# x loaded transposed, and the root and the shift of the first norm put on after the q, k and v products

## The chip, the cores and the metric

The kernel runs on one core of one Trainium2 chip. A core has five engines with a queue each: TensorE (PE, matrix products, with its weight loads counted apart as PEld), VectorE (DVE), ScalarE (ACT), GpSimd (POOL) and SyncE (SP), which here only issues DMA transfers. Data lie in SBUF (128 partitions); products land in the eight banks of PSUM. The metric is device microseconds of one execution. The kernel before takes 1100.62 us, the median of three runs between 1099.32 and 1101.92.

## The reference, cut to what matters

One decoder layer on a sequence of 1024 rows of width 1024, float32 throughout. The change concerns the start of its first half:

```python
mod = c_act @ w_ada[l] + b_ada[l]                    # c_act = silu(c), one vector
sh1, sc1, g1, sh2, sc2, g2 = split(mod, 6)
h = rmsnorm(x, pre_w_mix[l]) * (1.0 + sc1) + sh1     # rmsnorm: x * rsqrt(mean(x*x) + EPS) * w
proj = h @ w_in[l]
aq, ak, av, hq, hf, hi, hg = split(proj)             # 512, 128, 128, then 4 x 512 columns
...                                                  # rotary, windowed attention on aq, ak, av
...                                                  # gated recurrence on hq, hf, hi, hg
x = x + g1 * rmsnorm(concat([attn, rec]) @ w_out[l], post_w_mix[l])
h = rmsnorm(x, pre_w_mlp[l]) * (1.0 + sc2) + sh2
x = x + g2 * rmsnorm(square(relu(h @ w_up[l])) @ w_down[l], post_w_mlp[l])
```

For one row t of h this is h[t, :] = root[t] * (x[t, :] * a) + sh1, where root is a number for each row and a = pre_w_mix * (1 + sc1) and sh1 are vectors along the width. So h @ W = root[t] * ((x * a) @ W) + sh1 @ W.

## The kernel before, in words

**Tiles.** Rows come in eight tiles `tb` of 128, and two halves `th` of four tiles. The width comes in eight blocks `kb` of 128. PE contracts over partitions, so h is needed with the width on partitions: tiles `hh[kb][th]` of 128 x 512. Each float32 operand of a large product is split in a high part (`hi`, written by ACT rounded to fp32r) and a low part (`lo`, the rest, by DVE), and a product is three: hi*hi, hi*lo, lo*hi. One row tile of q takes 24 products 512 wide, one of k and v together 24 products 256 wide.

**Before the first product** (lines 103 to 220, 337 to 374): SP loads x row by row, ACT squares and sums it, POOL takes the power -1/2 (`norm_rstd`), DVE or ACT scales the rows (`norm_scale`), PE transposes 128 x 128 pieces into PSUM (`first_T`), and `split_evac` writes the high part scaled by a and shifted by sh1 on ACT, subtracts the shift again on POOL, and writes the low part from PSUM on DVE. The scale and shift vectors come from `wada1` in pieces (`mod_mm`, `mod_fold`), for the block or two blocks that are due next. PE fills waiting time at the start with products that nobody reads (`idle`, tile `spare`).

**The first half** (lines 406 to 455): for each block, the four row tiles of half 0 get part 0 (hi*hi and hi*lo of q and kv), then part 1 (lo*hi), in six PSUM banks. **The second half** (lines 620 to 639): half 1 is transposed and split, q of tile 4 is accumulated meanwhile, and the results of tiles 0 to 3 are read out (`qproj`, `kvproj`) and rotated (`rope`).

**Attention and values** (lines 642 to 679): a loop of 16 fillers, which are q and k of tiles 4 to 7 and then `values(0..7)`, the third of the other projections, on h; between them the steps of `attention(tb)` are issued, tile 0 from filler 4 on. After it the recurrence heads, the output projection and the channel mixing follow; they take some 900 us and are not touched.

**What sets the order.** Up to line 640 `pin(True, ...)` makes every engine issue in the order of the program text. From line 640 on a planner orders each engine's queue by the order of the text among what it holds ready, but nothing goes ahead of the last pinned instruction of its engine. SP is planned throughout. Pools with a fixed number of buffers (`H` 32 tiles, `W` 6, `T2` 5, PSUM `pmm` 2, `pb` 5, `pa` 1) make a new tile wait for the release of an old one.

Line numbers in the profile are mostly 39, the helper that issues every operation, so rows are read by tile names: `x`, `xT`, `pm` (modulation), `pq` and `pk` (q and k, v products), `pv` (values), `hhi` and `hlo`, `comb` (attention scores).

Of the kernel before, what the change touches and what calls it, by code (L numbers as in the profile page):

```python
# [9 lines left out]
F32 = mybir.dt.float32  # L10
# [6 lines left out]
P = 128  # L17
# [30 lines left out]
def hybrid_layer(ctx: ExitStack, tc: tile.TileContext, I, out, dbg=None):  # L48
# [54 lines left out]
    xh = [[None, None] for _ in range(TB)]  # L103

    def load_x(tb, hfs=(0, 1)):
        for hf in hfs:
            xh[tb][hf] = (m_ if tb < 4 else hT_)(f"x{tb}_{hf}")
            SP.dma_start(xh[tb][hf], I["x"][tb * P:(tb + 1) * P, hf * 512:(hf + 1) * 512])

    load_x(0)  # L110
# [3 lines left out]
    tab = cload("tab", [P, 200], pool=tiny0, eng=POOL)  # L114
# [15 lines left out]
    prew1s = small.tile([P, KB], F32, tag="prew1s", bufs=1, name="prew1s")  # L130
# [55 lines left out]
    ssx = [small.tile([P, 4, 2], F32, tag="ssx", name=f"ssx{th}") for th in range(2)]  # L186

    def norm_sq(tb, hfs=(0, 1), eng=None):
        for hf in hfs:
            junk = t_(f"jx{tb}_{hf}")  # L190
            if eng is DVE:
                DVE.tensor_tensor(junk, xh[tb][hf], xh[tb][hf], ALU.mult)
                DVE.tensor_reduce(ssx[tb // 4][:, tb % 4, hf:hf + 1], junk, AX.X, ALU.add)
                continue
            ACT.activation(junk, xh[tb][hf], AF.Square, accum_out=ssx[tb // 4][:, tb % 4, hf:hf + 1])

    rx = {}

    def norm_rstd(th, a, b):

        if not a:
            rx[th] = small.tile([P, 4], F32, tag="rr4", name=f"r_x{th}")
        t = small.tile([P, 4], F32, tag="rs4", name=f"t_x{th}{a}")
        for i in range(a, b):
            DVE.tensor_scalar(t[:, i:i + 1], ssx[th][:, i, 0:1], ssx[th][:, i, 1:2], D * EPS, ALU.add, ALU.add)
        POOL.tensor_tensor(rx[th][:, a:b], t[:, a:b], mhalf[:, a:b], ALU.pow)

    def norm_scale(th, hf, eng, tbs=range(4)):
        for tb in tbs:
            xt = xh[4 * th + tb][hf]  # L210
            if eng is ACT:
                ACT.activation(xt, xt, AF.Copy, scale=rx[th][:, tb:tb + 1])
            else:
                DVE.tensor_scalar(xt, xt, rx[th][:, tb:tb + 1], None, ALU.mult)

    def first_T(th, kb, mk=tp_ps):
        pst = mk(f"xT{th}_{kb}")
        hf, col = kb // 4, (kb % 4) * P
# [13 lines left out]
    hh = [[None, None] for _ in range(KB)]  # L232

    def first_evac(th, kb, pst, then=None):
        hh[kb][th] = (hT_(f"hhi{kb}_{th}", F32R), hT_(f"hlo{kb}_{th}", F32R))
        c = slice(kb, kb + 1)
        split_evac(pst, a1[:, c], sh1[:, c], ns1[:, c], *hh[kb][th], f"f{th}_{kb}", then)
# [27 lines left out]
    nc.vector.memset(sel, 0.0)  # L265
    for gate in range(2):
        gs = slice(64 * gate, 64 * gate + 64)
        nc.vector.memset(sel[gs, gs], 1.0 / 32)
# [12 lines left out]
    def mod_mm(q, kps=range(4)):  # L281

        n = 256 if q[0] else P
        if kps[0] == 0:
            pm[q] = a_ps(f"pm{q[0]}_{q[1]}")
        for kp in kps:
            for i in range(4):
                w2 = wa1[q, kp, i // 2][:, i % 2 * 256:][:, :256] if q[0] else wa1[q, kp, 0][:, P * i:P * i + P]
                PE.matmul(pm[q][32 * i:32 * i + 32, :n], lhsT=csr[:, 2 * kp + i % 2, :], rhs=w2,
                          start=(kp == 0), stop=(kp == 3), tile_position=(0, 32 * i))  # L290

    def mod_copy(q):
        n = 256 if q[0] else P
        pm[q, 0] = t_(f"ms{q[0]}_{q[1]}", (P, n))
        DVE.tensor_copy(pm[q, 0], pm[q][:, :n])

    def mod_fold(q):
        n = 2 if q[0] else 1
        pst, ms = pm[q], pm[q, 0]
        for j in range(n):  # L300
            PE.matmul(pst[:, 256 + P * j:256 + P * j + P], lhsT=ms[:, P * j:P * j + P], rhs=sel, start=True, stop=True)
        s2 = small.tile([P, 2], F32, tag="m1s", name=f"m1s{q[0]}_{q[1]}")
        cols = pst[:, 256:256 + n * P].rearrange("p (n g j) -> p g n j", g=2, j=64)[:, :, :, 0]
        c = slice(2 * q[0] + q[1], 2 * q[0] + q[1] + n)
        DVE.tensor_tensor(s2[:, :n], cols[:, 1], bT[:, 8 + c.start:8 + c.stop], ALU.add)
        DVE.tensor_tensor(sh1[:, c], cols[:, 0], bT[:, c], ALU.add)
        DVE.scalar_tensor_tensor(a1[:, c], s2[:, :n], 1.0, prew1s[:, c], ALU.add, ALU.mult)
        DVE.tensor_scalar(ns1[:, c], sh1[:, c], -1.0, None, ALU.mult)

    wa1, wqr, wkvr = {}, [], []  # L310

    def load_wa(q, kp, gate=0):
        src = I["wada1"][gate, q[0], kp] if q[0] else I["wada1"][kp % 2, 0, 2 * q[1] + kp // 2]
        wa1[q, kp, gate] = load_raw(hT_, f"wa{gate}_{q[0]}{q[1]}_{kp}", src)
# [1429 lines left out]
```

## Time and profile before

| | |
|---|---|
| median of three runs | 1100.62 us (1099.32 to 1101.92) |
| profiled execution, first to last instruction | 1097.6 us; no device time of its own is listed, the median is 3.0 us more than this span |
| PE busy | 1076.2 us, 98% |
| DVE, ACT, POOL busy | 795.1, 584.6, 373.2 us |
| first product of q | 15.91 us |
| first half of the projections ends | 63.5 us |
| tiles 4 and 5 done, first attention transpose | 84.5 us |
| first values product | 112.7 us |
| first product of the recurrence heads | 197.9 us |

The page gives busy time of each engine over the span. The timeline lists merged runs of equal instructions: start, length, engine, source line, operation, output and inputs, shape, count, and in brackets the idle time before them with what ended it. The rows that the prediction reads are shown there.

### The profile page before, as it was taken

Reading aid. Unit: us, or ns where it says so; the run is one execution under the profiler, and the core shown is the slowest. Engines: PE = TensorE matmul, PEld = TensorE weight load, DVE = VectorE, ACT = ScalarE, POOL = GpSimd, SP = SyncE. Lnnn points to the kernel's source line nnn. Section 1 sums busy time; section 2 is a strip of 40 time slices with the busy share of each in tenths; the row PEclk is TensorE's granted clock in tenths of the full one; section 3 lists DMA queues with packets and bytes.
Section 4 is the critical chain, followed back from the end, with each engine's and each line's share of the span. In section 5 each row is a group of like instructions: output and inputs, shape, how many; then the busy total and the mean of one; then the engine's idle time right before and its main releaser. Section 6 shows DMA issues by size and latency. Waiting matters only on the chain.

```text
span 1097.6 us, 16208 instructions
## 1 busy us (share of the span) xinstructions
PE 1076.2 (98%) x5547; PEld 878.2 (80%) x5547; DVE 795.1 (72%) x1323; ACT 584.6 (53%) x1206; POOL 373.2 (34%) x499
## 2 busy tenths in 40 slices
PE   8999999999999999999999999999999999999995
PEld 6788776778888888888888888888888888888884
DVE  4365777878865574559776767876767787899876
ACT  3445544364565764566655555556664543555434
POOL 1153211033324663432543444533333333310014
PEclk9999999999999999999999999999999999999998
DMA  9701301534310352324577676767998888998537
GB/s 347 265 7 57 117 1 43 181 101 140 125 56 11 108 182 96 125 79 144 194 246 249 233 259 227 257 216 244 320 364 289 275 299 259 337 308 272 169 76 131
DMA packets 101587, 203.37 MB, mean 185 GB/s; under 512 B 13025, under 2 KB 13681, under 8 KB 101505
## 3 DMA queue, kind: packets, MB, share of 16 engines
q1 hardware_dynamic: 85968, 154.52, 41.4%
q0 software_dynamic: 15392, 47.57, 14.3%
q8 instruction: 43, 0.70, 0.3%
q14 instruction: 40, 0.32, 0.1%
q10 hardware_dynamic: 144, 0.26, 0.1%
HBM read 147.25 MB, written 55.05 MB: 184 GB/s over the span
## 4 chain that ended last, share of the span: by engine, by line
PE 92%; DVE 3%; ACT 1%; DMA 1%; POOL 1%; issue 1%; SPq 0%; DVEq 0%; POOLq 0%; ACTq 0%
PE pda L39 16%; PE pua L39 14%; PE pdc L39 8%; PE po L39 8%; PE puc L39 7%; PE pu L39 4%; PE pdb L39 4%; PE pq L39 4%; PE phg L39 4%; PE phq L39 3%; PE pub L39 3%; PE phf L39 3%; PE pv L39 3%; PE pk L39 2%; PE o L39 1%; PE sc L39 1%
## 5 line engine op out<-in xcount | busy, mean ns | idle before, releaser
L39 POOL TENSOR_TENSOR b<-b,b 128x512 f32<-128x512 f32 x64 | 89.6, 1400 | 222.8 <-DMA b<-w_dn 222.4
L39 ACT ACTIVATE dw<-dwr 128x512 fp32r<-128x512 f32 x72 | 45.4, 630 | 46.5 <-DMA dwr<-td 32.4
L39 ACT ACTIVATE s<-s 128x512 f32<-128x512 f32 x84 | 53.0, 631 | 31.8 <-DVE s L39 30.5
L39 DVE TENSOR_TENSOR dw<-dwr,dw 128x512 fp32r<-128x512 f32 x72 | 53.6, 744 | 9.0 <-ACT dw L39 8.9
L39 DVE TENSOR_TENSOR acc<-pda,acc 128x512 f32<-128x512 f32 x68 | 46.5, 684 | 13.7 <-PE pda L39 13.3
L39 POOL DMA_DIRECT2D td<-b x64 | 36.3, 567 | 21.6 <-POOL b L39 18.7
L39 POOL TENSOR_TENSOR rrf<-ssf,mhalf 128x1 f32<-128x1 f32 x7 | 7.9, 1253 | 95.3 <-DVE ssf L39 95.3
L39 DVE TENSOR_TENSOR wt<-s,wt 128x512 fp32r<-128x512 f32 x42 | 37.2, 886 | 2.6 <-ACT wt L39 2.5
L39 ACT ACTIVATE s<-pua 128x512 f32<-128x512 f32 x28 | 16.7, 598 | 39.4 <-PE pua L39 33.9
L39 ACT ACT_TABLE_LOAD x28 | 35.9, 1283 | 1.2 <-PEq L1737 0.7
L39 DVE SCALAR_TENSOR_TENSOR macc<-wada,cs,macc 128x512 f32<-128x512 f32 x42 | 33.7, 803 | 3.4 <-DMA wada<-wada 2.9
L39 POOL DMA_DIRECT2D b<-w_dn x64 | 34.4, 540 | 0.0
L39 POOL TENSOR_TENSOR comb<-comb,rd 128x512 f32<-128x512 f32 x8 | 11.7, 1458 | 63.3 <-DVE rd L39 44.2
L39 PE MATMUL pua<-bt_0h,wt 128*128 128x512 f32 x84 | 32.7, 389 | 0.0
L39 PE MATMUL pua<-bt_1h,wt 128*128 128x512 f32 x84 | 32.7, 389 | 0.0
L39 PE MATMUL pua<-bt_3h,wt 128*128 128x512 f32 x84 | 32.7, 389 | 0.0
L39 PE MATMUL pua<-bt_2h,wt 128*128 128x512 f32 x84 | 32.7, 389 | 0.0
L39 DVE TENSOR_TENSOR wt<-a,wt 128x512 fp32r<-128x512 f32 x42 | 31.0, 738 | 0.9 <-ACT wt L39 0.9
L39 DVE TENSOR_TENSOR acc<-pdc,acc 128x512 f32<-128x512 f32 x36 | 24.6, 684 | 8.5 <-PE pdc L39 8.4
L39 ACT ACTIVATE wt<-s 128x512 fp32r<-128x512 f32 x42 | 26.3, 626 | 8.2 <-DVE s L39 8.0
L39 PE MATMUL pda<-dw,du_6h 128*128 128x512 f32 x96 | 29.6, 389 | 0.0
L39 PE MATMUL pda<-dw,du_7h 128*128 128x512 f32 x96 | 29.5, 389 | 0.0
(757 smaller groups left out, 3746.1 us busy)
## 6 DMA issues: line engine op xcount, KB each, us to landing
dur<-ud SPq DMA_DIRECT2D x112, 256.0 KB, 4.5
wada<-wada SPq DMA_DIRECT2D x64, 256.0 KB, 3.5
b<-w_dn POOLq DMA_DIRECT2D x64, 256.0 KB, 5.2
td<-b POOLq DMA_DIRECT2D x64, 256.0 KB, 3.3
dwr<-td SPq DMA_DIRECT2D x64, 256.0 KB, 4.3
a<-w_u SPq DMA_DIRECT2D x56, 256.0 KB, 4.4
dwr<-w_dn SPq DMA_DIRECT2D x48, 256.0 KB, 4.5
ud<-s SPq DMA_DIRECT2D x42, 256.0 KB, 3.6
```

The source lines that it names most:

```text
L39: ins = op(*args, **kw)
```

## The change

x comes from the host transposed as well (`xT`, blocks of 128 x 512), so it isn't transposed on PE. q, k and v are multiplied from x times a alone. The root of each row is put on when the products are read out of PSUM, and sh1 @ W is added as one row, the same for all tiles. Sums of squares run over partitions now, so ACT squares, POOL adds eight blocks and PE sums over partitions. The other projections (values and heads) still use h: half 0 is multiplied in place by rows of roots on POOL (`h_rows`) and split (`h_split`) late, half 1 is loaded once more for it. The scale vector is computed from `wsc`, half as many tiles, and the shift vector by DVE from `wada`. Tiles 4 and 5 are done together in the second half, so the loop of fillers has 12 instead of 16, with attention from filler 1 on.

The diff, cut to its core (a line of "..." where lines are left out):

```diff
-    load_x(0)
+    BLK = {0: 1, 1: 1, 2: 2, 4: 2, 6: 2}
+    scw = {b: [] for b in BLK}
+    xw = [w_(f"xT0_{i}") for i in range(4)]
+    xT = [[xw[kb // 2][:, kb % 2 * 512:kb % 2 * 512 + 512] for kb in range(KB)], [None] * KB]
...
+    load_sc(0)
+    load_x0(0)
...
-    tab = cload("tab", [P, 200], pool=tiny0, eng=POOL)
+    tab = cload("tab", [P, 200], pool=tiny0, eng=ACT)
...
+    def square_x(th, kb):
+        if kb == 0:
+            ssq[th] = m_(f"ssq{th}")
+            ACT.activation(ssq[th], xT[th][kb], AF.Square)
+        else:
+            sq = t_(f"sqx{th}_{kb}")
+            ACT.activation(sq, xT[th][kb], AF.Square)
+            POOL.tensor_tensor(ssq[th], ssq[th], sq, ALU.add)
+
+    def x_root(th):
+        pst = tp_ps(f"ssx{th}")
         for j in range(4):
-            PE.transpose(pst[:, j * P:(j + 1) * P], xh[th * 4 + j][hf][:, col:col + P], ident)
-        return pst
+            PE.matmul(pst[:, j * P:(j + 1) * P], lhsT=ssq[th][:, j * P:(j + 1) * P], rhs=ones, start=True, stop=True)
+        t = small.tile([P, 4], F32, tag="rs4", name=f"t_x{th}")
+        DVE.tensor_scalar(t, pst.rearrange("p (j c) -> p j c", c=P)[:, :, 0], D * EPS, None, ALU.add)
+        rx[th] = small.tile([P, 4], F32, tag="rx", name=f"r_x{th}")
+        POOL.tensor_tensor(rx[th], t, mhalf[:, 0:4], ALU.pow)
+        rx8[th] = small.tile([P, 4], F32, tag="rx8", name=f"r_x8{th}")
+        DVE.tensor_scalar(rx8[th], rx[th], 0.125, None, ALU.mult)
+
+    def x_rows(th):
...
+        DVE.tensor_tensor(d3, ident.unsqueeze(1).broadcast_to([P, 4, P]), rx[th].unsqueeze(2).broadcast_to([P, 4, P]),
+                          ALU.mult)
+        pst = tp_ps(f"rbx{th}")
+        for j in range(4):
+            PE.matmul(pst[:, j * P:(j + 1) * P], lhsT=ones, rhs=dg[:, j * P:(j + 1) * P], start=True, stop=True)
+        rxb[th] = raw_(f"rxb{th}")
+        ACT.activation(rxb[th], pst, AF.Copy)
...
+    def x_split(th, kb, then=None):
...
+        ACT.activation(hi, xT[th][kb], AF.Copy, scale=a)
+        if then:
+            then()
+        DVE.scalar_tensor_tensor(lo, xT[th][kb], a, hi.bitcast(F32), ALU.mult, ALU.subtract)
+
+    def h_rows(th, kb, eng=POOL):
+        eng.tensor_tensor(xT[th][kb], xT[th][kb], rxb[th], ALU.mult)
+
+    def h_split(th, kb):
...
+        split_evac(xT[th][kb], a1[:, c], sh1[:, c], ns1[:, c], hi, lo, f"f{th}_{kb}")
...
+    def add_sh(half, ks):
+        for k in ks:
...
+                DVE.scalar_tensor_tensor(sacc[half], wt, c, sacc[half], ALU.mult, ALU.add)
+
+    def fold_sh(half):
...
+            PE.transpose(pst[:, j * P:(j + 1) * P], sacc[half][:, j * P:(j + 1) * P], ident)
...
+    def shift_mm(kind):
+        if kind == "q":
+            DVE.tensor_copy(csr, sh1.unsqueeze(2).broadcast_to([P, KB, 32]))
+        n = 512 if kind == "q" else 256
...
+                PE.matmul(pst[32 * i:32 * i + 32, :n], lhsT=csr[:, k, :], rhs=w, start=(r == 0), stop=(r == 1),
+                          tile_position=(0, 32 * i))
+        shp[kind] = t_(f"shp{kind}", (P, n))
+        ACT.activation(shp[kind], pst[:, :n], AF.Copy)
+
+    def shift_fold(kind):
...
+            PE.matmul(pst[:, j:j + P], lhsT=sel, rhs=shp[kind][:, j:j + P], start=True, stop=True)
+        shb[kind] = hv_(f"shb{kind}")[:, :n]
+        ACT.activation(shb[kind], pst[:, :n], AF.Copy, scale=0.125 if kind == "q" else 1.0)
...
-    idle(15)
...
+    idle(6)
+    mod_mm(0)
+    mod_copy(0)
     idle(2)
...
+    mod_fold(0)
     idle(4)
...
     for kb in range(KB):
...
+        square_x(0, kb)
+        if kb and b:
+            mod_mm(b)
...
-        if kb + 1 < KB:
-            xT0.append(first_T(0, kb + 1))
...
+        if kb in (2, 3, 4, 5):
+            add_sh(0, range(2 * kb - 4, 2 * kb - 2))
         if kb == 6:
...
+            fold_sh(0)
+            load_sh(1, range(4))
+            for k in range(4, KB):
+                load_x1(k)
+            load_sh(1, range(4, KB))
+        if kb >= 5:
+            for k in ((0,), (1, 2), (3,))[kb - 5]:
+                square_x(1, k)
         if kb == 7:
...
+            x_root(0)
+            add_sh(1, range(4))
         for tb in range(4):
             first_mm(kb, tb, 1)
...
+        ACT.activation(q, pq, AF.Copy, scale=rx8[tb // 4][:, tb % 4:tb % 4 + 1])
...
+            DVE.tensor_scalar(kv, pk, r, None, ALU.mult)
...
+            DVE.scalar_tensor_tensor(kv, pk, r, shb["k"], ALU.mult, ALU.add)
...
+    def shift_q(tb):
+        POOL.tensor_tensor(qn[tb], qn[tb], shb["q"], ALU.add)
+
+    def shift_kv(tb):
+        POOL.tensor_tensor(kvn[tb], kvn[tb], shb["k"], ALU.add)
...
+    for kb in range(KB):
+        x_split(1, kb)
+        if kb == 0:
+            qproj(0)
+            qproj(1)
+            pq0 += [mm_ps("pq4"), mm_ps("pq5")]
+            pk45 = tp_ps("pk45")
+            pk0 += [pk45[:, 0:256], pk45[:, 256:512]]
+        if kb in (1, 2):
+            for tb in (2 * kb - 2, 2 * kb - 1):
+                kvproj(tb)
+        if kb == 1:
+            qproj(2)
+            qproj(3)
+        if kb < 4:
+            square_x(1, kb + 4)
+        if kb == 1:
+            x_rows(0)
+        if kb < 4:
+            add_sh(1, (kb + 4,))
+        if kb == 4:
+            fold_sh(1)
+        if kb == 5:
+            x_root(1)
+            shift_mm("q")
+            shift_mm("k")
+        if kb == 6:
+            shift_fold("q")
+            shift_fold("k")
+            x_rows(1)
+        if kb >= 3:
+            h_rows(0, kb - 3)
+        for part in range(2):
+            for tb in (4, 5):
+                first_mm(kb, tb, part)
+    for tb in range(4, 6):
+        qproj(tb)
+        kvproj(tb)
     for tb in range(4):
         eng = DVE if tb < 2 else POOL
+        shift_kv(tb)
+        rope(tb, 2, eng)
+        shift_q(tb)
         rope(tb, 8, eng)
-        rope(tb, 2, eng)
     pin(False, ACT, DVE, POOL, PE)

     def filler(i):
-        if i < 8:
-            (kvproj if i % 2 else qproj)(4 + i // 2)
-            rope(4 + i // 2, 2 if i % 2 else 8)
+        if i < 4:
+            (kvproj if i % 2 else qproj)(6 + i // 2)
+            if i == 0:
+                for kb in range(5, KB):
+                    h_rows(0, kb)
+            for kb in (2 * i, 2 * i + 1):
+                h_split(0, kb)
+            shift_q(4 + i)
+            rope(4 + i, 8)
+            rope(4 + i, 2)
+            if i == 3:
+                for k in range(KB):
+                    load_x1(k, hv_)
         else:
-            values(i - 8)
+            values(i - 4)
+            if i < 8:
+                for kb in (2 * i - 8, 2 * i - 7):
+                    h_rows(1, kb)
+                    h_split(1, kb)
...
-    att_a = (4, 5, 6, 7, 8, 9, 10, 11)
-    mod_a = (12, 13, 15)
-    for i in range(16):
+    att_a = (1, 2, 3, 4, 5, 6, 7, 8)
+    mod_a = (8, 9, 11)
+    for i in range(12):
```

More of the change, by code (lines that the diff above doesn't have):

```diff
@@ L183, in modrow @@
         POOL.tensor_tensor(t[:, hs], t[:, hs], wt, ALU.mult)
[L186 to L214, printed above, removed]
@@ L264, in hybrid_layer @@
     sel = XA.tile([P, P], F32, tag="sel", name="sel")
[L265 to L268, printed above, removed]
+    nc.vector.memset(sel, 1.0 / 32)
     def hv_(name):
```

258 lines of the change are left out of this document (119 added, 139 removed).

## The prediction

> **What bounds the kernel now.** I read the page first, then busy time by stage, then the merged timeline and the chain of waits of the first 85 us.
>
> ```profile
> span 1097.6 us, 16208 instructions
> PE 1076.2 (98%) x5547; PEld 878.2 (80%) x5547; DVE 795.1 (72%) x1323; ACT 584.6 (53%) x1206; POOL 373.2 (34%) x499
> 0.00:15.90 15.90, 12.54 (x71) 8.82 (x71) 6.47 (x26) 7.81 (x20) 2.76 (x8) 1.00 0.89 306
> 15.90:63.50 47.60, 47.59 (x370) 38.31 (x371) 20.77 (x52) 20.27 (x40) 7.53 (x10) 1.00 0.68 254
> 63.50:84.50 21.00, 20.39 (x124) 17.18 (x123) 12.82 (x37) 8.38 (x13) 15.25 (x39) 1.00 0.05 14
> 84.50:112.70 28.20, 27.86 (x216) 23.10 (x215) 18.86 (x43) 16.29 (x56) 9.23 (x21) 1.00 0.21 65
> ```
>
> The last four rows are stages (width; busy PE, weight load, DVE, ACT, POOL; granted clock; DMA). PE is the bound: from 15.9 us on it hardly pauses, so a change pays in two ways only: PE work that goes, and PE waits that come or go. POOL and DVE have room in the second row, and POOL is 15.25 of 21.0 in the third.
>
> **The start.** Timeline rows of PE, ACT and POOL, and the table of DMA issues:
>
> ```profile
> 1.65 5.99 PE L39 MATMUL spare<-spare,ones_r 128*128 128x512 f32 x15 [1.65 <-DVE spare L121]
> 9.08 2.31 PE L39 MATMUL spare<-spare,ones_r 128*128 128x512 f32 x9
> 13.06 0.64 PE L39 MATMUL pm<-wa,csr 128*32 128x128 f32 x16
> 15.91 0.50 PE L39 MATMUL pq<-wq0h,hhi 128*128 128x512 f32 x1 [0.38 <-ACT hhi L39]
> 3.40 0.63 ACT L39 ACTIVATE jx<-x 128x512 f32<-128x512 f32 x1 [1.16 <-DMA x<-x]
> 13.48 0.63 ACT L39 ACTIVATE wq0h<-wqr 128x512 fp32r<-128x512 f32 x1 [2.48 <-DMA wqr<-w_q]
> 1.31 0.73 POOL L39 DMA_DIRECT2D c_tab<-tab  x1 [0.86 <-POOLq L1737]
> c_tab<-tab POOLq DMA_DIRECT2D x1, 100.0 KB, 5.0
> ```
>
> The first tile is there at 3.40, wq0, the thirteenth on SP's queue, at 13.48: 0.84 a tile. After the change two scale tiles, one of x and wq0 lead, so wq0 is there at 3.40 + 3 x 0.84 = 5.9. `c_tab`, there at 1.31 + 5.0 = 6.3 now, moves to ACT's queue: between 3.4 (like the first tile) and 6.3; I take 4.0, since it shares the engines with two tiles. I allow 0.8 for the three small steps of silu: the first scale products start at 4.8, take one 0.64 row, and from the end of `pm` to the first `pq` it was 15.91 - 13.70 = 2.2. First product 7.6 instead of 15.9: **-8.3**, with 7.0 to 9.9 as its ends. Square sums, root and scaling of x leave this path; the squares move behind the products.
>
> Fifteen spare products took 0.40 each, nine later ones 0.26, at a granted clock of 1.00 in the rows: PE's first microseconds run slower. Twelve spare products and a gap replace 31. If that rate lasted as long after the new first product, the loss is at most 15 x 0.40 - 15 x 0.23 = 2.6; at least 0. I take **+0.6**, as most of the slow time is still spent on spares. [...]
>
> **The first half, 15.9 to 63.5.** Prices, from the chain of waits and the timeline:
>
> ```profile
> 18.03 1.01 PE pm L39 x32
> 22.25 1.00 PE pm L39 x16
> 27.44 0.45 PE pm L39 x4
> 27.89 0.44 PE xT L39 x4
> 73.31 2.88 PE pk L39 x24
> 76.19 5.47 PE pq L39 x24
> ```
>
> PE loses nine sets of transposes, 9 x 0.44 = 4.0; half of the modulation products, 0.5 in the second part (1.01) and 1.0 in each of three quarters (two rows like 22.25 become one), 3.5. It gains `fold_sh`, four transposes 0.44, and `x_root`, four full products at 0.45 / 2 = 0.22, 0.9. **-6.2**; the half ends at 7.6 + 0.6 + 41.4 = 49.6, not 63.5. DMA keeps ahead: 60 tiles were loaded here, 60 are now (16 scale, 16 shift, 16 x, 12 weights), and a block needs half the modulation tiles. DVE gets eight additions of the shift and POOL seven to ten of the squares: hidden, since a low part is due only 2.8 (eight `pq` at 5.47 / 24 = 0.23, eight `pk` at 0.12) after its block starts; uncovered, each is one of the rows below.
>
> **The second half, tiles 4 and 5, 63.5 to 84.5.** More prices:
>
> ```profile
> 34.20 2.56 ACT L39 ACTIVATE x<-x,r_x 128x512 f32<-128x512 f32 x4
> 211.31 3.11 DVE L39 SCALAR_TENSOR_TENSOR macc<-wada,cs,macc 128x512 f32<-128x512 f32 x4
> 8.82 0.69 DVE L39 TENSOR_TENSOR jx<-x 128x512 f32<-128x512 f32 x1
> 72.65 1.40 DVE L39 COPY kv<-pk 128x256 f32<-128x256 f32 x4
> 8.57 0.31 DVE L39 COPY csr<-cs 128x256 f32<-128x256 f32 x1
> 73.35 0.60 ACT L39 ACTIVATE q<-pq 128x512 f32<-128x512 f32 x1 [2.18 <-PE pq L39]
> 56.71 1.02 POOL L39 TENSOR_TENSOR r_x<-t_x,mhalf 128x4 f32<-128x4 f32 x1 [2.46 <-DVE t_x L39]
> L39 POOL TENSOR_TENSOR b<-b,b x64: 1282/1302/1965, 565.1 to 963.4; 128x512 f32<-128x512 f32 x64
> ```
>
> PE work: q and k of two tiles 2 x (5.47 + 2.88) = 16.7; two `x_rows` and `x_root` 2.7; `fold_sh` 0.4; `shift_mm` q at twice the 1.00 row, 2.0, and k 1.0; `shift_fold` six products, 1.35. 24.2. Then waits, all from orders pinned in the code:
> - `x_root(0)` stands before the last low-part products (1.4), and its read, power (1.02) and 1/8 take about 1.4. Only then does ACT read q0 (0.60) and free the bank of pq4: 0.6.
> - DVE has four shift additions (2.8) and the first low part (0.78) queued behind that root; PE gets to it after 0.6 + 1.4: 1.6.
> - `x_rows(0)` is ahead of block 1 on PE. Its diagonal stands on DVE behind one more addition, a low part and two kv reads: 0.78 + 0.78 + 0.70 + 0.69 - 0.70 of PE work = 2.2.
> - in block 5 `shift_mm` waits for root, 1/8 and `csr`: 0.2 + 1.02 + 0.2 + 0.31 = 1.7.
>
> That is 6.1. A sharing comes on top; POOL and DVE, timeline:
>
> ```profile
> 564.83 0.68 DVE L39 TENSOR_TENSOR wt<-s,wt 128x512 fp32r<-128x512 f32 x1
> 565.09 1.58 POOL L39 TENSOR_TENSOR b<-b,b 128x512 f32<-128x512 f32 x1 [3.96 <-DMA b<-w_dn]
> 565.55 1.67 DVE L39 TENSOR_TENSOR s<-a,s 128x512 f32<-128x512 f32 x1
> ```
>
> POOL's addition, 1.30 by the median, took 1.58 while a DVE instruction with two SBUF operands ran, and the next DVE one took 1.67 instead of 0.68, ending 0.55 after POOL. They exclude each other; DVE lost 1.0, POOL 0.28. Low parts read PSUM and SBUF before; now `x_split` reads x and the high part, both SBUF, as the shift additions do, while POOL adds squares and multiplies rows. Queue against queue: POOL's additions for blocks 4 and 5 fall into the second and third wait (+1.2 each), the next two and the first rows delay the low part of block 3 and the last shift addition (+0.5, +1.35). Waits 10.4, end at 49.6 + 24.2 + 10.4 = 84.2, against 80.0 without it. I take 84.2: the rows show it. So **+13.6** on the stage's 21.0. [...]
>
> **The attention stage, from 84.5.** Its PE work stays (28.2 to the first `pv`), but two banks now come free at once: **+0.6** for one ACT read. POOL is what runs late:
>
> ```profile
> 15.96 0.70 POOL L39 TENSOR_SCALAR f<-hhi,ns 128x512 f32<-128x512 f32 x1 [3.62 <-ACT hhi L39]
> 76.22 0.57 POOL L39 TENSOR_TENSOR rt<-q,c_cosT 128x128 f32<-128x128 f32 x1
> 78.57 0.25 POOL L39 TENSOR_TENSOR kv<-rt 128x32 f32<-128x32 f32 x1
> 80.31 0.95 POOL L39 MEMSET comb<- 128x1024 f32 x1
> 93.59 1.48 POOL L39 TENSOR_TENSOR comb<-comb,rd 128x512 f32<-128x512 f32 x1 [7.62 <-ACT q L39]
> 183.27 1.06 PE L39 MATMUL pT<-c_tab,comb 128*128 128x128 f32 x8 [0.42 <-DVE comb L39]
> 201.59 0.49 PE L39 MATMUL rb<-dg,ones 128*128 128x128 f32 x2 [0.45 <-DVE dg L39]
> 73.97 0.55 DVE L39 TENSOR_TENSOR rt<-q,c_cosT 128x128 f32<-128x128 f32 x1
> 77.23 0.20 DVE L39 TENSOR_TENSOR kv<-rt 128x32 f32<-128x32 f32 x1
> ```
>
> One tile's ropes take POOL 76.22 to 78.82, 2.6 (eight instructions). From the shift rows (4.5 before the second half ends, 79.7) it has four shifts of q and k (1.30, and half of it for the 256 columns of k: 4 x 1.95) and two ropes, 13.0; then three row products 3.9, eight `h_split` steps 5.6, three q shifts 3.9, three ropes 7.8, the memset 0.95 and two `comb` 3.0: 38.2, to 117.9, and 0.75 for the last low part, 118.6. The first values tile wants that one after 21 of its 24 products (4.8), at 84.2 + 0.6 + 28.2 + 4.8 = 117.8: 0.8 late. DVE's partners in that time, eight splits of whv (0.69), eight low parts (0.78) and its ropes (73.97 to 77.43), are 15.2. If POOL loses a quarter of it as above (0.28 of 1.28), 3.3: **+4.1**. Ends: 0.8, and 8.4 at a half. The memset that used to be early now stands behind 9 us of this queue, so the first attention tile, which writes into `comb`, starts late too; what is queued on DVE behind its predicated copy is the next tiles' maxima. ACT has eight or more splits (0.64 each, the row at 34.20), in 28.2 of which it is busy 16.3. Reloading half of x, 8 more tiles on SP's queue in the fourth filler, meets DMA at 0.21 and stands ahead of no load that is due sooner.
>
> The loop is four fillers shorter and the attention tiles start one filler later in it, so one values tile (5.5) less lies behind the last of them. At that end PE waited for DVE in the rows at 183.27 and 201.59. I take 0, since head products follow without a pause; without that cover it is up to 5.5.
>
> **Sum.** -8.3 + 0.6 - 6.2 + 13.6 + 0.6 + 4.1 = +4.4 on the profiled 1097.6, which is 3.0 below the median 1100.62: **1105.0**. The 900 us after are the same text; I add nothing.
>
> **Rivals.**
> - *The gain survives* (faster): queue order alone costs 6.1 and POOL's queue 0.8. -8.3 + 0.6 - 6.2 + 9.3 + 0.6 + 0.8 = -3.2, 1097.4. For it: DVE is busy only 12.8 of 21.0; against it: the 1.67 row, and the same queues are fuller now. It decides if POOL's additions fall between DVE's.
> - *Gain spent, no more* (same): second half as forecast, but attention absorbs the 4.1, as other PE work is at hand (four q and k products, 16.7). 1100.9.
> - *POOL's queue becomes the bound* (clearly slower): 8.4 instead of 4.1, and the slow first rate costs 2.0 instead of 0.6: 1110.7; with `c_tab` at 6.3 or a bare end of the stage it is more, up to 1116. For it: 38 us of POOL before the first values tile; against it: unpinned instructions may be put ahead of one another. [...]
> - *It doesn't do what it says*: `c_tab` late takes 2.3 off the start; a part of each case.
>
> **Chances.** Forecast 0.44 (own range 1102 to 1109), gain survives 0.26, spent 0.16, bound 0.14. A measurement of this kernel tells about 0.2%, 2.2 us. Of the forecast 0.02 lies within it: slower 0.56, same 0.18, faster 0.26. The range 1095.5 to 1112 leaves the tails of the first and the last rival out, some 0.15 together.
>
> **What would show it.** Right: first `pq` near 7.6; tile 3 of the first half done near 50; PE waits for DVE's low part and diagonal in the blocks 0 and 1 of the second half, and for `csr`; POOL unbroken from 80 to 115 and PE waiting for `hlo` at the first `pv`. Wrong: POOL rows at 1.3 and DVE rows at 0.7 side by side, the second half over by 80, or `pv` starting with hlo ready.

## The result and the profile after

The changed kernel takes **1140.41 us** (median of five, 1138.24 to 1142.06), the kernel before 1099.83 (median of five on the same chip; the 1100.62 above is of three): ratio **1.0363**, 95% interval 1.0351 to 1.0376. It is 40.6 us slower; the forecast was 1105.0 and a range to 1112. The profiled execution has a span of 1137.2, 39.6 more than 1097.6.

The page's first part, then the busy time by stage of the changed kernel (start and end, width; busy PE, weight load, DVE, ACT, POOL; granted clock; DMA):

```profile
PE 1078.1 (95%) x5466; PEld 877.5 (77%) x5466; DVE 830.5 (73%) x1335; ACT 593.2 (52%) x1208; POOL 431.8 (38%) x538
```

```profile
0.00:15.90 15.90, 12.78 (x93) 8.91 (x94) 6.85 (x20) 6.87 (x12) 0.50 (x5) 1.00 0.91 323
...
84.50:112.70 28.20, 15.32 (x94) 12.31 (x94) 14.95 (x35) 9.66 (x15) 27.57 (x44) 0.78 0.03 10
112.70:130.00 17.30, 12.19 (x67) 9.81 (x66) 12.48 (x22) 6.99 (x26) 16.04 (x26) 0.70 0.23 62
130.00:168.00 38.00, 32.88 (x211) 23.99 (x209) 28.83 (x60) 22.27 (x76) 15.08 (x23) 0.99 0.37 118
168.00:198.00 30.00, 27.05 (x190) 19.25 (x190) 23.52 (x53) 16.76 (x56) 9.60 (x13) 1.00 0.00 1
198.00:240.00 42.00, 35.89 (x182) 24.11 (x183) 37.33 (x72) 16.34 (x53) 5.61 (x7) 0.96 0.25 78
240.00:300.00 60.00, 59.33 (x342) 48.36 (x341) 43.59 (x75) 30.75 (x52) 17.73 (x20) 1.00 0.39 127
```

PE is busy about as long as before (1078.1 against 1076.2), so the 40 us are waits. Up to 84.5 the waits are about paid for by the earlier start; what is lost lies between 84.5 and 240, and PE is full again from there. POOL is busy 43.6 of the 45.5 us up to 130.

What PE waits for there are the attention tiles. Each of the eight tiles masks its scores into `comb` with four predicated copies on DVE. The rows give all 32, before and after (minimum, median and longest in ns, then the start of the first and of the last):

```profile
core 0 of [0], span 1097.6 us
...
L39 DVE COPY_PREDICATED comb<-c_mle,sc x32: 431/442/454, 86.5 to 173.4; 128x256 f32<-128x256 int32 x32
```

```profile
core 0 of [0], span 1137.2 us
...
L39 DVE COPY_PREDICATED comb<-c_mle,sc x32: 389/437/453, 110.1 to 213.1; 128x256 f32<-128x256 int32 x32
```

The first is 23.6 late, the last 39.7. Over the seven tiles between them the pace went from 86.9 / 7 = 12.4 us to 103.0 / 7 = 14.7. From the last copy to the end it is 924.2 before and 924.1 after. So **the whole loss is there at the last mask copy: 23.6 of a late start and 16.1 of a slower pace.**

This pace is a mean. From the first copy of a tile to that of the next it was 9.2, 12.7, 13.8 and then 12.5 to 12.6 before; it is 14.7, 17.8, 13.8, 14.3 and then 13.5 to 13.6 after. So 10.6 of the 16.1 are lost in the first two steps.

Timeline rows around the first copy, in the changed kernel:

```profile
101.09 0.95 POOL L39 MEMSET comb<- 128x1024 f32 x1
107.75 0.69 POOL L39 TENSOR_SCALAR f<-hhi,ns 128x512 f32<-128x512 f32 x1
108.41 4.18 POOL L39 TENSOR_TENSOR xT<-xT,rxb 128x512 f32<-128x512 f32 x3
...
108.47 1.74 DVE L39 SCALAR_TENSOR_TENSOR hlo<-xT,a,f 128x512 fp32r<-128x512 f32 x1 [4.39 <-POOL f L39]
110.14 1.43 DVE L39 COPY_PREDICATED comb<-c_mle,sc 128x256 f32<-128x256 int32 x4
...
110.30 0.60 ACT L39 ACTIVATE qT<-pqT 128x512 f32<-128x512 f32 x1 [12.90 <-DVE hlo L39]
...
96.31 1.16 PE L39 MATMUL sc<-kT,qT 64*128 64x128 f32 x16
97.41 0.66 PE L39 MATMUL pqT<-c_tab,q 128*128 128x128 f32 x4
110.62 0.48 PE L39 MATMUL pkT<-c_tab,kv 128*128 128x128 f32 x1 [12.56 <-DVE comb L39]
```

Tile 0's scores were ready at 96.31 + 1.16 = 97.5. The copies stood on DVE behind a low part `hlo` of the second making of h (the products and splits that make h from x once more for the values and heads), which waited 4.39 for POOL's subtraction `f`; POOL came to that `f` at 107.75. ACT's copy of tile 1's queries waited 12.90 and PE 12.56, both released by DVE. POOL then put row products of the *second* half, which no values tile before the fifth needs, ahead of the next `f`.

### The profile page after: what moved, and what is told of

Its sections match the earlier page's. It is cut to its first block, busy times and chain, and to the rows that moved or that the text cites. A ratio compares the mean times of both kernels' runs of the same rounds, so it can differ in the third digit from the quotient of the medians.

```text
span 1137.2 us, 16136 instructions
## 1 busy us (share of the span) xinstructions
PE 1078.1 (95%) x5466; PEld 877.5 (77%) x5466; DVE 830.5 (73%) x1335; ACT 593.2 (52%) x1208; POOL 431.8 (38%) x538
## 4 chain that ended last, share of the span: by engine, by line
PE 76%; DVE 8%; POOL 5%; DMA 5%; ACT 3%; issue 2%; SPq 0%; DVEq 0%; POOLq 0%; ACTq 0%
PE pda L39 15%; PE pua L39 13%; PE pdc L39 8%; PE po L39 7%; PE puc L39 7%; PE pu L39 4%; PE pdb L39 4%; PE phg L39 3%; PE pub L39 3%; PE phq L39 3%; PE phf L39 2%; ACT comb L39 1%; DMA xT<-xT 1%; DMA sh<-wada 1%; PE o L39 1%
## 5 line engine op out<-in xcount | busy, mean ns | idle before, releaser
L39 POOL TENSOR_TENSOR b<-b,b 128x512 f32<-128x512 f32 x64 | 92.1, 1439 | 218.9 <-DMA b<-w_dn 218.5
L39 DVE TENSOR_TENSOR acc<-pda,acc 128x512 f32<-128x512 f32 x68 | 46.5, 684 | 13.1 <-PE pda L39 12.9
L39 POOL TENSOR_TENSOR ssq<-ssq,sqx 128x512 f32<-128x512 f32 x14 | 19.9, 1428 | 43.6 <-ACT sqx L39 43.5
L39 ACT ACTIVATE comb<-comb,nm 128x128 f32<-128x128 f32 x64 | 24.8, 388 | 20.0 <-DVE nm L39 13.8
L39 DVE TENSOR_TENSOR s<-puc,s 128x512 f32<-128x512 f32 x14 | 9.7, 690 | 28.8 <-issue 26.3
```

The costliest lines, as they stand in the source:

```text
L39: ins = op(*args, **kw)
```

## The experiments

All are edits of the changed kernel; e12, e13 and e14 leave steps out and so compute something else. A median is of two executions (e12 three, e13 six, e14 ten), each ratio is to executions of the kernel before beside them (medians 1099.2 to 1100.4), and the copies are of one profiled execution. The last column is the span less the start of the last mask copy.

| kernel | median us | ratio to before (95%) | first and last mask copy | rest |
|---|---|---|---|---|
| before | 1099.83 | 1 | 86.5, 173.4 | 924.2 |
| changed | 1140.41 | 1.0363 (1.0351 to 1.0376) | 110.1, 213.1 | 924.1 |
| e1_order | 1137.94 | 1.0347 (1.0317 to 1.0377) | 110.8, 214.2 | 922.7 |
| e2_fused | 1126.10 | 1.0239 (1.0209 to 1.0269) | 99.3, 201.0 | 922.9 |
| e3_memset | 1141.20 | 1.0376 (1.0346 to 1.0407) | 113.9, 216.5 | 922.9 |
| e4_half2 | 1137.20 | 1.0340 (1.0310 to 1.0370) | 108.9, 212.2 | 923.0 |
| e5_start | 1132.42 | 1.0294 (1.0264 to 1.0324) | 95.5, 207.3 | 923.5 |
| e6_all | 1119.47 | 1.0176 (1.0147 to 1.0206) | 96.8, 196.4 | 921.8 |
| e7_allstart | 1118.77 | 1.0170 (1.0140 to 1.0200) | 92.0, 194.5 | 923.6 |
| e8_early | 1115.86 | 1.0146 (1.0117 to 1.0176) | 96.7, 191.1 | 923.1 |
| e9_earlyp | 1125.57 | 1.0234 (1.0205 to 1.0264) | 98.6, 202.2 | 922.3 |
| e10_fix | 1114.16 | 1.0126 (1.0097 to 1.0156) | 93.0, 189.7 | 922.3 |
| e11_fixw | 1115.80 | 1.0141 (1.0110 to 1.0173) | 93.9, 194.8 | 920.6 |
| e12_nosplit | 1109.75 | 1.0090 (1.0068 to 1.0113) | 97.0, 187.8 | 920.2 |
| e13_nosplit2 | 1103.98 | 1.0035 (1.0020 to 1.0050) | 92.5, 182.2 | 921.7 |
| e14_noshift | 1102.23 | 1.0018 (1.0008 to 1.0029) | 85.1, 176.3 | 923.4 |

The rest is 920 to 924 in all sixteen, while the last copy moves by 43. A kernel's time can be read off that one row, to some 4 us.

### e1_order: POOL's order

```diff
+            if i == 3:
+                POOL.last = fins["f0_7"]      # nothing goes ahead of the last subtraction f of half 0
+            for tb in ((4,), (5,), (), (6, 7))[i]:
+                shift_q(tb)
+                rope(tb, 8)
+                rope(tb, 2)
```

> Same work, other order on POOL: the shift and rope of tiles 6 and 7, the row products of the second half and the bias rows may not go ahead of the last subtraction f of the first half. In the changed kernel's trace these steps take about 13 us of POOL's queue between the first f at 99.23 and the last at 122.14. Theory ORDER (POOL's steps stand in the wrong order, and VectorE and ScalarE, which work in order, stand behind f): the last f comes near 110, the first value product near 120 instead of 132, and the kernel takes 1126 to 1131. Theory LOAD (POOL has too much to do whatever the order): what is put back is late in its turn, 1137 to 1142. Theory MEMSET (the first score tile waits for the fill of its tile at 101.09 and the order of the rest is idle talk): 1138 to 1142.

ORDER's forecast of 1126 to 1131 missed. First product of each of the eight values tiles (start of the first and of the last), in the changed kernel and in this run, and then POOL's third `f` in this run:

```profile
L39 PE MATMUL pv<-whv0h,hhi x8: 389/389/505, 132.1 to 218.0; 128*128 128x512 f32 x8
```

```profile
L39 PE MATMUL pv<-whv0h,hhi x8: 388/394/476, 124.6 to 218.1; 128*128 128x512 f32 x8
```

```profile
108.14 1.35 POOL L39 TENSOR_SCALAR f<-hhi,ns 128x512 f32<-128x512 f32 x2
```

The first values product comes 7.5 earlier and the last at the same time. So **the first values product, by which the prediction priced this stage, is not what the end hangs on.** The mask copies tell it, and they did not move (110.8, 214.2). The run does not clear POOL's order ahead of the first copy, though: the `f` that this copy stands behind came at 108.14, no earlier than the 107.75 of the changed kernel.

### e2_fused: POOL's load

```diff
-        eng.tensor_tensor(xT[th][kb], xT[th][kb], rxb[th], ALU.mult)      # h_rows, POOL
-        split_evac(xT[th][kb], ...)                                      # f on POOL
+        DVE.scalar_tensor_tensor(t, t, a1[:, c], rxb[th], ALU.mult, ALU.mult)
+        ACT.activation(hi, t, AF.Identity, bias=sh1[:, c])
+        DVE.scalar_tensor_tensor(lo, t, sh1[:, c], hi.bitcast(F32), ALU.add, ALU.subtract)
```

> POOL's load taken away: the row product and the subtraction f (16 of 1.25 and 16 of 0.68 on POOL, 31 us) are left out of POOL; VectorE makes x times scale times root in one step and the low part from it in a second, so VectorE gets 16 more steps of about 0.75, 12 us. Same output. Theory LOAD: POOL's queue from 81.43 to 128 falls by some 20 us, the first value product comes near 112 to 115 and the kernel takes 1110 to 1120. Theory ORDER: also faster, since no f is left to stand behind, 1110 to 1125; this run alone does not part LOAD from ORDER, the run with the order does. Theory MEMSET: the fill moves up only by the 3.74 us of row products ahead of it, 1133 to 1140. Rival VECTOR (VectorE becomes the bound, since it was 89 per cent busy from 198 to 240): 1125 to 1140 with VectorE above 90 per cent in the stage.

14.3 us less, the most of any single edit that computes everything, but less than LOAD and ORDER said: the time lies in VECTOR's range. The copies start 10.8 earlier; the pace is still 101.7 / 7 = 14.5. What POOL lost, DVE has. A stage of this run, and then the busy time from 84 to 228 in the kernel before, the changed one and this run:

```profile
84.50:112.70 28.20, 22.38 (x134) 19.14 (x134) 26.00 (x54) 13.94 (x36) 27.48 (x46) 0.88 0.12 33
```

```profile
84.00:228.00 144.00, 139.79 (x843) 104.48 (x842) 108.41 (x224) 71.93 (x227) 30.60 (x52) 1.00 0.24 77
```

```profile
84.00:228.00 144.00, 116.50 (x717) 86.33 (x715) 105.79 (x220) 68.63 (x220) 73.32 (x109) 0.92 0.17 53
```

```profile
84.00:228.00 144.00, 124.78 (x729) 91.13 (x728) 124.79 (x254) 70.94 (x226) 52.34 (x82) 0.93 0.21 64
```

DVE is busy 26.00 of 28.20, and over the longer stretch 108.4, 105.8, 124.8; POOL 30.6, 73.3, 52.3. In both versions of the change more is to be done beside the tiles than before.

### e3_memset: the fill alone

```diff
+    comb0 = w_("comb0", (P, 2, 2, 2, P))
+    POOL.memset(comb0.rearrange("p a g m j -> p (a g m) j"), NEG)   # ahead of the shift and rope tail
```

> One step moved: the fill of the first score tile goes ahead of the shift and rope tail on POOL, into POOL's idle stretch of 4.63 us before 81.43. Theory MEMSET (the fill at 101.09 holds the first attention tile, whose key transposition then waits 12.56): the first mask copy follows the first scores, the first value product comes 10 to 15 us earlier, 1125 to 1131. Theories ORDER and LOAD: the mask copies stand behind hlo on VectorE, which waits for f at 107.75, so nothing or 1 to 3 us, 1136 to 1141.

MEMSET falls: the fill ran at 77.9 and the copies came at 113.9, if anything later. In the changed kernel they wait for DVE's queue, not for the fill. The fill is next in line: where no `f` holds DVE up, in e2 and e12, the first copy waited 2.1 and 2.3 for it.

### e4_half2: the waits of the second half

```diff
+            x_split(1, 0)             # in block 7 of the first half, ahead of x_root(0)
...
-        x_split(1, kb)
+        if kb + 1 < KB:
+            x_split(1, kb + 1)
...                                    # diagonal one block ahead of x_rows, shift products in block 6, not 5
```

> Second half of the q, k, v products alone: the split of a block is made one block ahead, the diagonal of the roots one block ahead of the products that spread it, and the shift's products stand one block later behind their column copy. In the changed kernel PE waited there 0.5, 2.06, 2.86 and 2.81 us and ran at half rate for some 4 us behind the third. Theory PREDICTED (these waits are the 10.4 us of the second half in my sum): they fall to 2 us or less in all, the second half ends at 77 to 80 instead of 85. What follows: by LOAD or ORDER POOL's queue sets the end and starts when the shift's rows are read, so the kernel gains only as far as these come earlier, 0 to 4 us, 1134 to 1140; if PE's end of the second half set the end instead, the whole 6 to 8 us come through, 1130 to 1134.

First product of query tile 6 in this run; it was at 86.29 in the changed kernel (shown below):

```profile
82.75 0.50 PE L39 MATMUL pq<-wq0h,xhi 128*128 128x512 f32 x1 [0.32 <-ACT q L39]
```

The half ends 3.5 earlier, not 5 to 8: the wait for the diagonal grew to 3.9. The kernel takes 3.2 less, but the interval of the ratio overlaps that of the changed kernel, so a gain this small isn't shown.

### e5_start: the start of the chain

```diff
-    att_a = (1, 2, 3, 4, 5, 6, 7, 8)
+    att_a = (0, 1, 2, 3, 4, 5, 6, 7)
...
+        if not tb:
+            ACT.last, DVE.last = qins.ins, cins.ins    # tile 0's query read-out and last mask copy
...                                                     # and the early fill
```

> Only the start of the attention chain is moved: the score tile's fill ahead of the shift and rope tail on POOL, the first attention tile traced one slot earlier, and no split of h on ScalarE or VectorE ahead of tile 0's query read-out and mask copies. All work stays. Theory CHAIN (the eight attention tiles are one serial chain; the first mask copy came at 110.14 against 86.51 before, 23.6 late, and the tiles follow 14.7 us apart instead of 12.4, another 16; these two make the 40 us): the first mask copy comes near 92 to 95, the last near 196 to 200, the first head product near 211 to 215 instead of 227.7, and the kernel takes 1123 to 1129. Theory LOAD (POOL has too much to do for the whole stage): the first copies come early, the later ones wait for POOL as before, 1134 to 1140.

```profile
core 0 of [0], span 1130.8 us
...
L39 DVE COPY_PREDICATED comb<-c_mle,sc x32: 382/440/448, 95.5 to 207.3; 128x256 f32<-128x256 int32 x32
```

8.0 us less, between the two theories. The first copy moved by 14.6, the last by 5.8: the pace worsened to 111.8 / 7 = 16.0. An earlier start alone is mostly lost again: from tile 0's first copy to tile 1's it is 22.0 us here (95.5 to 117.5), 14.7 in the changed kernel.

### e6_all and e7_allstart: together

```diff
+            DVE.scalar_tensor_tensor(q, pq, r8, shb["q"], ALU.mult, ALU.add)    # tiles 4 to 7, instead of ACT and POOL
...                                    # with the edits of e2, e3, e4; e7 also with those of e5
```

> Four edits together: the row product and the subtraction f off POOL as in the fused run, the fill early, the second half of the products reordered, and the shift of the query tiles 4 to 7 added on VectorE as they are read out of PSUM instead of on POOL (4 of 1.29 us). Theory CHAIN: the first mask copy moves from 99.3 in the fused run to about 93, by the 4.6 us of waits that the reordered half saved up to the shift rows and the fill that no longer stands on POOL; kernel 1117 to 1122. Theory LOAD: POOL falls by another 5 us in the stage, 1116 to 1121; the two are parted by the run with the start alone.

> The four edits and the early start together. Theory CHAIN: first mask copy near 88 to 90, pace 13 to 14.5 us a tile, last copy near 182 to 190, kernel 1104 to 1113. If the pace comes back to 12.4 it is 1096 to 1100; if VectorE, with 26 of 28.2 us busy behind 84.5 in the fused run, can't take the start and the splits at once, 1113 to 1120.

Four edits bring 20.9 us, as expected (both theories gave that range); the early start on top of them nothing more (0.7, inside the uncertainty). The forecast of 1104 to 1113 for e7 was wrong, the one for a DVE that can't take both (1113 to 1120) right: the copies start at 92.0, 4.8 earlier than in e6, and end 1.9 earlier.

### e8_early, e10_fix: the first half's h made under the products

```diff
+        if kb >= 4:                              # second half of the products; e8: from block 3, the last four in block 7
+            for k in (2 * kb - 8, 2 * kb - 7):
+                nxt = h_split(0, k)
...
-            for kb in (2 * i, 2 * i + 1):        # in the fillers
-                h_split(0, kb)
...                                              # e10 also: the column copy csr ahead of the second roots
```

> The run before (four edits and the early start) with the splits of the first half's h moved up from the attention stage into the second half of the products, where VectorE was busy 8 of 21 us: eight row and eight low-part steps of 0.75, 12 us of VectorE and 6 of ScalarE, lie there under the products. The diagonal of the first roots also stands right behind the roots. Theory CHAIN WITH VECTOR (a tile's serial chain waits in VectorE's order behind the splits; 27 of 28 us busy after 84.5): the tiles come 12.5 to 13.5 us apart instead of 14.5, 7 to 12 us less, 1106 to 1112. Rival LATENCY (the pace is the chain's own length, whatever lies beside it): 1116 to 1120. Rival SECOND HALF (the moved steps delay the products there by as much as they free later): 1114 to 1122 with the second half ending 5 us later or more.

> The run with the first half's splits moved up, with two of its steps set right in the second half: the splits spread two a block over its last four blocks, and the shift's column copy ahead of the second roots. There the read-out of query tiles 4 and 5 stood 6.75 behind the last low parts, and the shift products 1.8 and 2.5. Theory CHAIN: the chain of tiles starts earlier by these waits, first mask copy near 88 to 90 instead of 96.7, the pace stays near 13.3, so 1106 to 1111. Rival PACE (the tiles' pace is set by VectorE's 26 of 28 us and an earlier start only lengthens the wait of the second tile, as from 110.1 to 95.5 in the run with the start alone, which brought 8 of 14.6 us): 1111 to 1115.

In e8 the read-out of query tiles 4 and 5 stood behind the moved steps, and PE with it:

```profile
89.65 0.80 PE L39 MATMUL pq<-wq0h,xhi 128*128 128x512 f32 x1 [6.75 <-DVE q L39]
```

That product came 5.7 later than in e7 (83.96), so the rival SECOND HALF was right: 2.9 less (the intervals overlap), not 7 to 12, though the pace came down from 14.6 to 13.5. Mended in e10, the first copy moved by 3.7, the last by 1.4, and 1.7 us came of it, less than the uncertainty: the rival PACE. e10, at 1.0126, has the lowest median of the versions that still compute everything; the intervals of e8 and e11 overlap its own.

### e9_earlyp, e11_fixw: work given back to POOL

```diff
+        if th:                                   # e9: half 1 has its rows and f on POOL again
+            eng.tensor_tensor(xT[th][kb], xT[th][kb], rxb[th], ALU.mult)
...
+                whv.append(load_split(g_, f"whv{kb}", I["w_hv"][kb], eng=POOL if kb % 2 else DVE))     # e11
```

> The same, with the second half's row product and subtraction f back on POOL (8 of 1.25 and 8 of 0.68, 15.5 us) and one low-part step on VectorE instead of two, 6 us off VectorE. POOL was busy 13 of 55 us from 112.7 to 168 in the run before, so it has the time. Theory CHAIN WITH VECTOR: 2 to 5 us less than its neighbour without this, 1102 to 1109. Rival POOL'S ORDER (VectorE again stands behind f, and POOL's row products behind a transfer): 2 to 8 us more than the neighbour.

> The same, and the low parts of every second block of the values' weights on POOL instead of VectorE (4 of 0.68 us on VectorE, 4 of about 1.25 on POOL). Theory CHAIN WITH VECTOR: 1 to 4 us less than its neighbour, 1103 to 1109. Rival POOL'S ORDER (POOL's split stands ahead of its share of a tile's score product): 1 to 6 us more than its neighbour.

```profile
core 0 of [0], span 1124.5 us
...
L39 DVE COPY_PREDICATED comb<-c_mle,sc x32: 427/439/447, 98.6 to 202.2; 128x256 f32<-128x256 int32 x32
```

e9 takes DVE's work away and is 9.7 us slower: pace 14.8 instead of 13.5. It adds more than the 2 to 8 that POOL'S ORDER gave. e11 brings nothing. Why steps on POOL cost more here than on DVE stays open. In the trace of e9 POOL put five row products, 6.25 us from 102.37, ahead of a tile's rotation; but it stood idle 6.9 to 10.5 us ahead of the later tiles' products on `comb`, so its load alone isn't the reason.

### e12_nosplit, e13_nosplit2: no second making of h

```diff
-        return [(hs[k][tb // 4][0][:, sl], hs[k][tb // 4][1][:, sl]) for k in range(KB)]
+        return [(xa[k][1][0][:, sl], xa[k][1][1][:, sl]) for k in range(KB)]
...                                    # no h_rows, no h_split, no second load of x
```

> The changed kernel with the second making of h left out, both halves: no row products, no second split, no second load of x; the values and the head projections read the scaled x of the second half instead, for all tokens (so they compute something else). 31 us of POOL, 12 of VectorE and 12 of ScalarE go. All runs so far have their span 921 to 924 us behind the start of the last mask copy, so the last copy is what is forecast. Theory CHAIN WITH LOAD (start and pace of the tiles are set by what the second making puts in the order of VectorE, ScalarE and POOL): first copy near 97 to 100, pace 12.4 to 13, last copy 184 to 190, kernel 1108 to 1114. Rival PACE OF ITS OWN (the tiles follow at 14.5 whatever lies beside them, because the cover of the query and key products is spent): last copy near 199 to 202, kernel 1123 to 1127.

> The four edits and the early start, with the second making of h left out in the same way. Theory CHAIN WITH LOAD: first copy near 89 to 91, pace 12.4 to 12.8, last copy 176 to 181, kernel 1099 to 1105: about the time before, so that the whole of what is lost beyond it is the second making. Rival PACE OF ITS OWN: last copy near 191 to 194, kernel 1115 to 1118, as in the run with the splits. If the start's gain of 8.3 came through, it would be under 1097.

```profile
core 0 of [0], span 1108.0 us
...
L39 DVE COPY_PREDICATED comb<-c_mle,sc x32: 399/440/449, 97.0 to 187.8; 128x256 f32<-128x256 int32 x32
...
96.96 1.44 DVE L39 COPY_PREDICATED comb<-c_mle,sc 128x256 f32<-128x256 int32 x4 [2.27 <-POOL comb L39]
```

```profile
core 0 of [0], span 1103.9 us
...
L39 DVE COPY_PREDICATED comb<-c_mle,sc x32: 396/440/453, 92.5 to 182.2; 128x256 f32<-128x256 int32 x32
```

CHAIN WITH LOAD held in both times and in the copies of e12; those of e13 came 1.5 (the first, 92.5) and 1.2 (the last, 182.2) after its bounds. The pace is 13.0 and 12.8 instead of 14.7 and 14.6, so the rival PACE OF ITS OWN falls. **Making h a second time costs some 30 of the 40.6 us** (1140.41 less 1109.75 is 30.7; the ratios give 30.0). In the spans it is 13.1 of the 23.6 of late start, 12.2 of the 16.1 of pace, and 3.9 behind the last copy. With the four edits and the early start in place it still costs 14.8 (1118.77 less 1103.98). The edit takes everything out at once, the steps on POOL, DVE and ACT and the second load of x; their shares aren't told apart.

### e14_noshift: the rest

```diff
+    for tb in range(2):                  # tiles 0 and 1, ahead of qproj(4), with no shift_kv and no shift_q
+        rope(tb, 2, DVE)
+        rope(tb, 8, DVE)
...
-    for tb in range(4):
+    for tb in range(2, 4):
         shift_kv(tb)
```

> The kernel with the four edits, the early start and without the second making of h, and now also without the shift of query, key and value tiles 0 and 1 (not added, so these compute something else); their rotation on VectorE then stands ahead of the read-out of tiles 4 and 5 and waits for no shift row. Theory LATE START (what is left of the loss, 4.8 us, is the chain's later start: first mask copy 92.5 against 86.5 before, since the shift rows are read at 81 and POOL adds them): first copy near 85 to 87, the last 174 to 177, kernel 1096 to 1099. Rival COVER (the tiles have less product work beside them than before, whatever the start: 17 instead of 25 us of query and key products): first copy early, last copy 179 or later, kernel 1101 to 1104.

```profile
core 0 of [0], span 1099.7 us
...
L39 DVE COPY_PREDICATED comb<-c_mle,sc x32: 431/440/449, 85.1 to 176.3; 128x256 f32<-128x256 int32 x32
```

The copies answer as LATE START said (85.1, 176.3), the median as COVER said. The first copy is 7.4 earlier than in e13, that of e13 4.5 earlier than in e12 (the edits of e7), and that of e12 13.1 earlier than in the changed kernel: with these three the late start is gone. In time 1.8 us come of it, but the interval overlaps that of e13, and 1.8 remain over the kernel before, with a first copy 1.4 earlier than there and a pace of 13.0 against 12.4. COVER's premise was wrong, though: in the kernel before and in this run the four fillers of tiles 6 and 7 are all the query and key products beside the tiles, not 25 us of them before. The pace differs only at its start: the steps from tile 1 to 2 and from 2 to 3 take 15.7 and 14.6 here, 12.7 and 13.8 before, and from then on they are 12.5 to 12.6 in both, with PE full (busy 37.99 of the 38 us from 130 to 168 in both). What holds those two steps stays open.

## Why the prediction was wrong

Rows of the changed kernel for the steps up to the first values product, from the timelines:

```profile
7.22 0.63 ACT L39 ACTIVATE wq0h<-wqr 128x512 fp32r<-128x512 f32 x1 [2.96 <-DMA wqr<-w_q]
8.51 0.50 PE L39 MATMUL pq<-wq0h,xhi 128*128 128x512 f32 x1 [1.20 <-ACT xhi L39]
8.85 0.39 PE L39 MATMUL pq<-wq0l,xhi 128*128 128x512 f32 x1
9.07 0.39 PE L39 MATMUL pq<-wq0h,xhi 128*128 128x512 f32 x1
...
51.21 0.50 PE L39 MATMUL pq<-wq0h,xhi 128*128 128x512 f32 x1 [0.50 <-ACT q L39]
54.94 0.50 PE L39 MATMUL pq<-wq0h,xlo 128*128 128x512 f32 x1 [2.06 <-DVE xlo L39]
58.77 2.05 PE L39 MATMUL rbx<-dgx,ones 128*128 128x128 f32 x8 [2.86 <-DVE dgx L39]
74.47 1.92 PE L39 MATMUL pshq<-wqr,csr 128*32 128x512 f32 x16 [2.81 <-DVE csr L39]
86.29 0.50 PE L39 MATMUL pq<-wq0h,xhi 128*128 128x512 f32 x1 [0.32 <-ACT q L39]
...
132.00 0.28 PE L39 MATMUL pk<-wkv3h,xlo 128*128 128x256 f32 x1
132.12 0.39 PE L39 MATMUL pv<-whv0h,hhi 128*128 128x512 f32 x1
...
54.15 0.74 DVE L39 SCALAR_TENSOR_TENSOR xlo<-xT,a,xhi 128x512 fp32r<-128x512 f32 x1
64.49 1.77 DVE L39 SCALAR_TENSOR_TENSOR xlo<-xT,a,xhi 128x512 fp32r<-128x512 f32 x1
```

- **Start, -8.3: right, 0.9 short.** First product 8.51, not 7.6; `wq0` was there at 7.22 instead of 5.9, and PE waited 1.20 for the high part of x, which ACT made behind the split of `wq0`.
- **Slow first rate, +0.6: not there.** The products follow 0.34 and then 0.22 apart.
- **First half, -6.2: right.** It ends at 51.21 - 0.50 = 50.7, forecast 49.6; the 0.9 of the start is in that.
- **Second half, +13.6: right in the places, in part by luck in the sum.** The forecast was 24.2 of work and 10.4 of waits, 34.6; it took 86.29 - 0.32 - 50.7 = 35.3. All four waits stand where they were put, each smaller: 0.50 (0.6), 2.06 (1.6 + 1.2), 2.86 (2.2 + 1.2) and 2.81 (1.7 and the last two queue terms), 8.2 in all. Work took 2.9 more than forecast, and 1.9 of that has no term in the sum: behind the third wait the eight spreading products and the eight after them took 4.18 us (58.77 to 62.95), the same sequence later 2.29 (80.72 to 83.01). The sharing of POOL and DVE is there: a low part takes 1.77 beside POOL's additions, and 0.74 at 54.15, when POOL stood idle up to 54.69. Two reads of `pk` out of PSUM took 0.87 together beside POOL's addition (62.76), and 0.86 with POOL idle (57.16).
- **Bank of pq, +0.6: right**, 0.32.
- **Attention stage, +4.1: the step that failed.** Up to here the sum came to about +1.8 and the forecast to +0.3; the span grew by 39.6, so this term was about 38. Three sentences of it failed:
  - "The first values tile wants that one ... at 117.8: 0.8 late" took the wrong consumer. POOL's queue was priced by when the values need it. The sign that was named for this being wrong came: the first `pv`, at 132.12, followed the last `pk` products without a pause and waited for no `hlo`. And e1 shows that moving it by 7.5 changes nothing at the end. The consumer that counts is tile 0's mask copy, in DVE's queue behind the low parts that wait for POOL.
  - "The memset that used to be early now stands behind 9 us of this queue, so the first attention tile ... starts late too" saw the late start and gave it no price, and the wrong cause (e3). It is 23.6, of which 13.1 go with the second making (e12).
  - "At that end PE waited for DVE ... I take 0" priced only the end of the stage. The tiles' pace has no term at all, so it was held at the old one. It went up by 2.3 a tile, 16.1 in all; e12 shows that 12.2 of these go when the sixteen further splits of h on ACT and DVE, and 31 us of POOL ahead of them, leave the queues that the tiles use.
- **Rivals.** *POOL's queue becomes the bound* had the place and the sign, 1110.7, but priced it by the same consumer. Its counter-argument, that unpinned instructions may be put ahead of one another, turned round: POOL put row products of the second half ahead of `f` of the first. *The gain survives* failed: even with the four edits and without the second making (e13) the kernel is 1.0035 of the one before. *Gain spent, no more* failed with the forecast: the stage didn't absorb its delay, it grew by 38. In *it doesn't do what it says*, `c_tab` was not late: ACT read it at 4.05, forecast 4.0.

## What to carry to other kernels

Work that moves behind a product isn't only to be added up on its engine; ask which serial chain stands in the same engine's queue, and price the delay by the chain's first and last step, not by the consumer of the moved work. Where one row (here the last mask copy) keeps a constant distance to the end in every variant, follow that row. Making an operand twice to get the first product early has to be paid for in engines that a chain may be waiting for: here the 7.4 us won at the start were spent in the waits of the second half, and the tiles began 23.6 later.

## What the runs showed of the hardware that was not expected

The mean granted clock was lower in three stretches in which PE had long waits: 0.77 from 50 to 65, with the first three waits of the second half in it, and 0.78 and 0.70 in the two stages from 84.5 to 130. It was 1.00 from 168 to 198, where PE was busy 90%, and also from 65 to 84.5, with the wait of 2.81 in it. Behind the waits of 2.06 and 2.86, with 1.0 us of products between them, eight products of 128 x 128 took 2.05, and the same eight took 1.06 later:

```profile
50.00:65.00 15.00, 9.57 (x45) 7.88 (x44) 11.87 (x17) 8.16 (x14) 4.99 (x5) 0.77 0.01 2
```

```profile
80.72 1.06 PE L39 MATMUL rbx<-dgx,ones 128*128 128x128 f32 x8
```

Together with the eight products that follow them, they took 4.18 us at a mean granted clock of 0.53 (58.77 to 62.95), and later 2.29 at 1.00 (80.72 to 83.01): 1.9 us more at the lower clock. What a lower clock cost in the attention stage stays open, as no run here takes the clock apart from the waits.
